# Another order of products in the feed-forward part of a two-layer transformer kernel, float32 on one core

## The chip, the cores and the metric

The kernel runs on one core of a Trainium2 chip. The core has a matrix engine (TensorE; PE in the profile, with its weight loads as PEld), two engines that work on rows of 128 partitions (VectorE, called DVE, and ScalarE, called ACT), a general one (GpSimd, called POOL), and SyncE (SP), which here only asks for transfers. Each engine takes its instructions strictly in order; they wait for each other by semaphores. Transfers (DMA) are asked for on a queue of SP or of POOL and carried out by 16 DMA engines that all queues share.

The metric is the device time of one execution in microseconds, the median of the runs.

## The reference, cut to what matters

All arrays are float32. There are two layers (DEPTH = 2); the sequence is S = 512 rows, the width D = 1024, the hidden width FFN = 2816. The change touches only the second half of each layer, the feed-forward network (FFN):

```python
for l in range(DEPTH):
    ...                                  # token mixer: three branches, gates, w_out
    x = layer_norm(ALPHA * x + mix, ln1_g[l], ln1_b[l])

    u = einsum('bsd,df->bsf', x, w_ffn_in[l])          # 512 x 1024 by 1024 x 5632
    u_gate, u_up = split(u, 2, axis=-1)
    ffn = einsum('bsf,fd->bsd', silu(u_gate) * u_up, w_ffn_out[l])   # 512 x 2816 by 2816 x 1024
    x = layer_norm(ALPHA * x + ffn, ln2_g[l], ln2_b[l])
```

## The kernel before, in words

**Numbers as pairs.** A float32 operand is carried as a pair of rounded float32r tiles, hi and lo. hi is a cast on ACT (L106 or L108 for activations, L154 or L259 for weights), lo = x − hi is a subtraction on DVE (L112 or L114, L155 or L260). A product of two pairs takes three matmuls (`mm3`, L121 to L124): hi·hi, hi·lo, lo·hi.

**Weights.** A weight block of 128 x 2048 floats (1 MB) is loaded into one of four staging buffers `st` (NSTAGE = 4), then cast and subtracted into one of three pairs `wh`, `wl` (AHEAD = 3). `run_items` fetches the weights of later items while fewer than three pairs are ready or in use. A staging buffer comes free when the subtraction has read it (and, where it keeps a running sum, after its last use); a pair when the last matmul of its product is done.

**Seven products.** Most of the FFN is done in blocks by a Strassen-Winograd scheme with seven products instead of eight: m1, y, x, m2, v, g, h (`u_two`, from L728). Each is 24 matmuls (two column halves j, four contraction tiles, three matmuls). x, g and h add onto the PSUM banks in which m1 was made, one after the other, v onto those of y. What a bank holds after g is read on DVE (`gg`, L760: `c = c22 - bank`), and only then may h write the same bank. The weights are sums of quarters of a weight matrix. `Chain` makes them one after the other in one staging buffer: SP loads (L174), and POOL adds the next quarter with an accumulating DMA (L178) as soon as the last sum has been split. `Close` keeps two or three quarters loaded (a, d, e) and adds on DVE (L233, L239). `ahead_a` and `ahead_c` ask for a weight early; they are called from the groups of an item (below).

**Stages.** The hidden columns are 22 tiles of 128. Sixteen come from four first-stage problems p, q, r, u (`u_fin`; Chain, Close, Chain, Close) of 512 gate and 512 up columns each. `gate_half` (L1200: tanh on ACT L1202, then DVE L1203) and `gated` (DVE L1211) make silu(gate)·up. `s_turn` (L1214) turns the result by eight PE transposes into two banks (L1223) and copies them on ACT (L1225). `s_ready`, `s_differ`, `s_sums`, `s_rest` (class `Twins`, L292 to L332) form the sums that the second stage takes as its other operand, a pair for each product, by casts and DVE operations (L322, L324 among them). The second stage has two output groups o and w (`fout_items`, both Chain) over four pairs of tiles each; their banks are added to the residual z by `plus` (L1295 the first time, L1297 later). The z tiles are loaded again from memory in o's m1 (`load_res`, eight loads of 256 KB).

The other six tiles (16 to 21) are plain: `u_ffn_first` (16, 17) and `u_ffn` (18 to 21), 48 matmuls each, and `ffn_done` (L1190) does tanh, gate and the split into a pair `hid[i]` at once. `fout_rest(0)` and `fout_rest(1)` multiply them by the last rows of w_ffn_out into the left and right 512 output columns. `fout_rest(0)` is two items, one for each weight block, with four banks open over both; `fout_rest(1)` (`chase`) takes both blocks, row tile by row tile, and each row tile's normalisation follows it.

**Order.** The order of products is a list written by hand (L1363 to L1379) of pairs (weights, function) with groups of further work. `run_items` (L550) issues an item's matmuls and, through `between`, one group after each of its halves. So the list sets the order of issue; a scheduler then fixes a static order on each engine, and that order is what runs.

Of the kernel before, what the change touches and what calls it, by code (L numbers as in the profile page):

```python
# [15 lines left out]
ALU = mybir.AluOpType  # L16
# [40 lines left out]
def trunk(ctx, tc, x_in, xT_in, w_in, ret_norm_g, da_norm_g, lq1, lk1, lq2, lk2, w_a, w_b, w_c, b_merge, w_out,  # L57
# [25 lines left out]
    def bank(name="ps"):  # L83
        return psp.tile([P, 512], F32, tag="ps", name=name)
# [276 lines left out]
    def proj_N(act, wts, t, ps, k0=0, start=True, stop=True):  # L361

        sl = slice(P * t, P * t + P)
        rows = [(wt, k) for wt in wts for k in range(wt.nk)]
        for i, (wt, k) in enumerate(rows):
            a = act[k0 + i]
            mm3(ps, a.hi[:, sl], a.lo[:, sl], wt.hi[:, k], wt.lo[:, k], start and i == 0, stop and i == len(rows) - 1)
# [84 lines left out]
    def bcast_rows(src):  # L452

        r = [g(name="bc") for _ in range(2)]
        for hf in range(2):
            nc.sync.dma_start(r[hf], src[:, 512 * hf:512 * hf + 512].to_broadcast([P, 512]))
        return r
# [145 lines left out]
    def layer(l):  # L603
# [586 lines left out]
        def ffn_done(i, pg, pu):  # L1190
            t = g(name="fth")
            nc.scalar.activation(t, pg, AF.Tanh, scale=0.5)
            nc.vector.scalar_tensor_tensor(t, t, 1.0, pg, op0=ALU.add, op1=ALU.mult)
            nc.vector.tensor_mul(t, t, pu)
            hid[i] = Pair("hid")
            split(hid[i], t, scale=0.5)

        nat, half = {}, {}

# [14 lines left out]
        def s_turn(pb, hf):  # L1214

            def fn():
                rows = [nat.pop((pb, 2 * hf + j)) for j in range(2)]
                for fp in range(2):
                    ps = bank("ph")
                    for i in range(2):  # L1220
                        for j in range(2):
                            o, c = 256 * i + P * j, P * (2 * fp + i)
                            nc.tensor.transpose(ps[:, o:o + P], rows[j][:, c:c + P], ident)  # L1223
                    t = half[pb, hf, fp] = g(name="hf")
                    nc.scalar.activation(t, ps, AF.Copy, scale=0.5)  # L1225
            return fn
# [3 lines left out]
        def s_ready(gi, fp):  # L1230
            def fn():
                pa, pc, k = 2 * gi, 2 * gi + 1, 8 * gi + 2 * fp
                tw = twins[gi, fp] = Twins(half.pop((pa, 0, fp)), half.pop((pa, 1, fp)))
                tw.ready(half.pop((pc, 0, fp)))
                hid[k], hid[k + 1] = tw.each
            return fn

        def s_differ(gi, fp):
            def fn():
                twins[gi, fp].difference(half.pop((2 * gi + 1, 1, fp)))  # L1240
            return fn

        def s_sums(gi, fp):
            def fn():
                twins[gi, fp].sums()
            return fn

        def s_rest(gi, fp):
            def fn():
                twins.pop((gi, fp)).rest()  # L1250
            return fn

        def s_x1(k):
# [29 lines left out]
        def u_ffn(i):  # L1283
            def fn(wt):
                pg = proj_T(x1T, wt, 0)
                pu = proj_T(x1T, wt, P)
                ffn_done(i, pg, pu)
            return [ffn_spec(i)], fn

        def plus(t, hf, ps, op, final=False):  # L1290

            z = x1["z"][t][hf]
            if (t, hf) in x2["fresh"]:
                x2["fresh"].remove((t, hf))
                nc.vector.scalar_tensor_tensor(z, z, ALPHA, ps, op0=ALU.mult, op1=op)  # L1295
            else:
                nc.vector.tensor_tensor(z, z, ps, op=op)  # L1297
            if final:
                x2["n"].stats(t, hf)

        def fout_items(gi):

            r0, kh = GROUPS[gi]
            hv = Chain(w_ffn_out[l], r0, kh)
            w = {}

            def it(name, *adds):
                def fn(wt):
                    if name == "m1" and gi == 0:
                        load_res(saved[2 * l])  # L1310
                        x2["fresh"] = {(t, hf) for t in range(NT) for hf in range(2)}
                    on = {"x": "m1", "g": "m1", "h": "m1", "v": "y"}.get(name, name)
                    for j in range(2):
                        w[on, j] = product([hid[r0 + k] for k in range(kh)], name, j, wt, w.pop((on, j), None))
                        for i, hf, op in adds:
                            plus(2 * i + j, hf, w[on, j], op)
                        if name in ("m2", "v", "h"):
                            w.pop((on, j))
                return [getattr(hv, name)], fn

            add, sub = ALU.add, ALU.subtract
            return {"c": hv.ahead_c, "m1": it("m1", (0, 0, add)), "y": it("y", (1, 1, add)), "x": it("x", (0, 1, sub)),
                    "m2": it("m2", (0, 0, add)), "v": it("v", (0, 1, add)), "g": it("g", (1, 1, sub)), "h": it("h", (1, 0, add))}

        def fout_rest(hf):


            banks = {}
            specs = rows_of(w_ffn_out[l], 512 * hf, REST, FT - REST)

            def block(kb):
                def fn(wt):
                    if kb == 0:
                        x2["n"] = Norm(x1["z"], v["g2"], v["b2"], bcast_rows(ln2_g[l:l + 1]),
                                       bcast_rows(ln2_b[l:l + 1]), xTs[l + 1], out if last else saved[2 * l + 1], xfs[l + 1])
                        banks[0] = [bank("pf") for _ in range(NT)]
                    end = kb == len(specs) - 1
                    for t in range(NT):
                        proj_N(hid, [wt], t, banks[0][t], REST + 4 * kb, kb == 0, end)
                        if end:  # L1340
                            plus(t, 0, banks[0][t], ALU.add, True)
                return fn

            def chase(*wts):
                n = x2["n"]
                for t in range(NT):
                    ps = bank("pf")
                    proj_N(hid, wts, t, ps, REST)
                    if t in (1, 2) and not last:
                        n.transposes(t - 1)  # L1350
                    plus(t, 1, ps, ALU.add, True)
                    if last:
                        n.finish(t)
                    else:
                        n.normalise(t)
                        if t == 2:
                            n.to_T(0)

            return [([sp], block(kb)) for kb, sp in enumerate(specs)] if hf == 0 else [(specs, chase)]

        p, q, r, u = u_fin(0, Chain), u_fin(1, Close), u_fin(2, Chain), u_fin(3, Close)
        o, w = fout_items(0), fout_items(1)
        for (specs, fn), *groups in [  # L1363
            (u_ffn_first([16, 17]), [s_natural(0)], [s_x1(0)]), (p["m1"], [s_x1(1)], [s_x1(2)]),
            (u_ffn(18), [s_x1(3), s_natural(1)], [p["c"]]), (p["m2"], [s_natural(2)], [s_natural(3)]), (p["y"],),
            (p["v"], [q["a"]]), (u_ffn(19),), (p["x"],), (q["m1"],), (p["g"], [s_turn(0, 0)]), (p["h"],),
            (q["y"], [q["c"]]), (q["v"], [s_turn(0, 1)]), (q["m2"],), (q["x"],), (r["m1"],), (q["g"], [s_turn(1, 0)]), (q["h"],),
            (r["y"],), (r["m2"], [s_turn(1, 1)], [r["c"]]), (r["v"], [u["a"]]), (r["x"],), (u["m1"],), (r["g"], [s_turn(2, 0)]),
            (r["h"], [s_ready(0, 0)], [s_ready(0, 1)]),
            (u["y"], [u["c"]]), (u["v"], [s_turn(2, 1)]), (u["m2"],), (u["x"],),  # L1370
            (o["m1"], [s_differ(0, 0)], [s_differ(0, 1)]), (u["g"], [s_turn(3, 0)]), (u["h"], [s_sums(0, 0)], [s_sums(0, 1)]),
            (o["m2"],), (o["y"], [s_turn(3, 1)], [o["c"]]), (u_ffn(20), [s_rest(0, 0)], [s_rest(0, 1)]), (o["v"], [s_ready(1, 0)], [s_ready(1, 1)]),
            (o["x"],), (w["m1"], [s_differ(1, 0)], [s_differ(1, 1)]), (o["g"],), (o["h"], [s_sums(1, 0)], [s_sums(1, 1)]),
            (w["m2"], [s_rest(1, 0)], [s_rest(1, 1)]), (w["y"], [w["c"]]), (u_ffn(21),), (w["v"],), (w["x"],),
            (w["g"],), (w["h"],),
        ]:
            item(specs, fn, *groups)
        for it in fout_rest(0) + fout_rest(1):
            item(*it)  # L1379

        def hook(b):
            x2["n"].transposes_of(1, b)
# [56 lines left out]
```

## Time and profile before

| | us |
|---|---|
| median of 3 runs | 1890.52 (1889.6 to 1891.29) |
| profiled execution, its own time | 1891.41 |
| its span | 1889.6 |
| window 602 to 940 (FFN of layer 0): PE busy | 333.69 of 338.00 |
| window 1542 to 1882 (FFN of layer 1): PE busy | 334.96 of 340.00 |
| window 1882 to 1889.6 (behind the last matmul): PE busy | 0.00 of 7.60 |

The profile is of one execution. Busy time of an engine is the time in which it executes; a wait is put down to the instruction whose semaphore came last. In the rows, `out<-in` gives tiles by the program's names, L is a line of the kernel, and `[2.43 <-DVE tc L760]` behind an instruction says that its engine had been idle for 2.43 us and that L760 on DVE ended the wait. The row of an item in the list of waits reads: who waited, for whom, us in total, how many times, the longest. The granted clock (PEclk) is a share of full speed. Matmuls overlap in the pipeline: one lasts 0.39 us, and the next starts 0.23 us after it.

### The profile page before, as it was taken

The numbers are of one execution on the slowest core, as the hardware profiler recorded it, in microseconds if no ns is written. First come the engines' busy times: TensorE is split into PE (matmuls) and PEld (weight loads), VectorE is DVE, ScalarE is ACT, GpSimd is POOL, SyncE is SP. The second block draws the span as 40 slices with busy tenths as digits, with TensorE's granted clock in tenths as the row PEclk, the third lists the DMA queues.
The fourth block names the chain that finished last, engine by engine and source line by source line (L and its number), as shares of the span: only waits on it lengthen the run. The fifth ranks groups of instructions, "written<-read, shape, count | busy, mean of one in ns | idle before, by whom it ended". The sixth has DMA issues, their size and how long they took to land. (4 is left out here: it accounts for less than half of the span.)

```text
span 1889.6 us, 24024 instructions
## 1 busy us (share of the span) xinstructions
PE 1869.7 (99%) x9138; PEld 1573.4 (83%) x9138; DVE 1344.3 (71%) x2055; ACT 973.5 (52%) x1579; POOL 124.4 (7%) x149
## 2 busy tenths in 40 slices
PE   9999999999999999999999999999999999999998
PEld 7888888888888888778898888888888888887786
DVE  6767756577766876688687778566776668757886
ACT  5545545566634454554255546455766345445540
POOL 2000000000001001010010000000000010010100
PEclk9999999999999999999999999999999999999999
DMA  9585443432155668698366944533322646686971
GB/s 287 164 280 144 122 162 107 123 122 69 57 183 142 152 192 201 170 231 205 129 194 171 285 112 135 167 114 99 123 68 82 194 115 174 174 212 189 220 191 45
DMA packets 220851, 297.69 MB, mean 158 GB/s; under 512 B 8516, under 2 KB 115104, under 8 KB 220736
## 3 DMA queue, kind: packets, MB, share of 16 engines
q1 hardware_dynamic: 192512, 241.20, 38.4%
q0 software_dynamic: 28224, 54.95, 17.1%
q8 instruction: 72, 1.18, 0.3%
q14 instruction: 43, 0.35, 0.1%
HBM read 273.00 MB, written 23.12 MB: 157 GB/s over the span
## 5 line engine op out<-in xcount | busy, mean ns | idle before, releaser
L122 PE MATMUL pt<-xTh,wh 128*128 128x512 f32 (+1 forms) x1072 | 397.2, 372 | 0.4 <-ACT wh L154 0.4
L123 PE MATMUL pt<-xTl,wh 128*128 128x512 f32 (+1 forms) x1072 | 393.5, 367 | 1.9 <-DVE xTl L112 1.9
L124 PE MATMUL pt<-xTh,wl 128*128 128x512 f32 (+1 forms) x1072 | 393.6, 368 | 0.0
L260 DVE TENSOR_TENSOR wl<-st,wh 128x2048 fp32r<-128x2048 f32 x126 | 288.3, 2289 | 143.5 <-ACT wh L259 143.3
L259 ACT CAST wh<-st 128x2048 fp32r<-128x2048 f32 x126 | 241.1, 1913 | 181.5 <-PE pf L124 91.1
L155 DVE TENSOR_TENSOR wl<-st,wh 128x1024 fp32r<-128x1024 f32 (+1 forms) x204 | 219.1, 1094 | 82.5 <-ACT wh L154 76.3
L154 ACT CAST wh<-st 128x1024 fp32r<-128x1024 f32 (+1 forms) x204 | 188.3, 949 | 161.4 <-PE pf L124 58.9
L123 PEld LDWEIGHTS pt<-xTl,wh 128*128 128x128 f32 x1072 | 202.3, 189 | 34.1 <-DVE xTl L112 2.3
L124 PEld LDWEIGHTS pt<-xTh,wl 128*128 128x128 f32 x1072 | 202.0, 188 | 33.7
L122 PEld LDWEIGHTS pt<-xTh,wh 128*128 128x128 f32 x1072 | 202.0, 189 | 33.0 <-ACT wh L154 1.0
L122 PE MATMUL pf<-wh,xTh 128*128 128x512 f32 x336 | 132.4, 394 | 6.1 <-DVE tc L760 4.9
L123 PE MATMUL pf<-wl,xTh 128*128 128x512 f32 x336 | 131.6, 392 | 0.0
L124 PE MATMUL pf<-wh,xTl 128*128 128x512 f32 x336 | 131.6, 392 | 0.0
L122 PE MATMUL pf<-wh,s43h 128*128 128x512 f32 x224 | 88.5, 395 | 0.0
L122 PE MATMUL pf<-wh,s12h 128*128 128x512 f32 x224 | 87.5, 391 | 0.0
L123 PE MATMUL pf<-wl,s43h 128*128 128x512 f32 x224 | 87.3, 390 | 0.0
L124 PE MATMUL pf<-wh,s43l 128*128 128x512 f32 x224 | 87.3, 390 | 0.0
L123 PE MATMUL pf<-wl,s12h 128*128 128x512 f32 x224 | 87.3, 390 | 0.0
L124 PE MATMUL pf<-wh,s12l 128*128 128x512 f32 x224 | 87.1, 390 | 0.0
L122 PEld LDWEIGHTS pf<-wh,xTh 128*128 128x128 f32 x336 | 63.5, 189 | 21.6 <-ACT wh L259 5.7
L745 ACT COPY tc<-pf 128x512 f32<-128x512 f32 x84 | 47.6, 588 | 60.5 <-PE pf L124 53.8
L124 PEld LDWEIGHTS pf<-wh,xTl 128*128 128x128 f32 x336 | 63.5, 189 | 13.3
(317 smaller groups left out, 3704.8 us busy)
## 6 DMA issues: line engine op xcount, KB each, us to landing
st<-in_w_in SPq DMA_DIRECT2D x60, 1024.0 KB, 5.2
st<-in_w_ffn_in SPq DMA_DIRECT2D x36, 1024.0 KB, 6.4
st<-in_w_ffn_in POOLq DMA_DIRECT2D x24, 1024.0 KB, 9.0
st<-in_w_ffn_out SPq DMA_DIRECT2D x20, 1024.0 KB, 6.5
st<-in_w_in SPq DMA_DIRECT2D x32, 512.0 KB, 5.2
st<-in_w_ffn_out POOLq DMA_DIRECT2D x16, 1024.0 KB, 9.0
st<-in_w_in POOLq DMA_DIRECT2D x12, 1024.0 KB, 10.9
th<-th SPq DMA_DIRECT2D x48, 256.0 KB, 5.0
```

The source lines that it names most:

```text
L122: nc.tensor.matmul(ps, lh, rh, start=start, stop=False, skip_group_check=onto)
L123: nc.tensor.matmul(ps, lh, rl, start=False, stop=False, skip_group_check=onto)
L124: nc.tensor.matmul(ps, ll, rh, start=False, stop=stop, skip_group_check=onto)
L154: return [nc.scalar.copy(self.hi[:, a:b], self.st[:, a:b]), nc.vector.tensor_sub(self.lo[:, a:b], self.st[:, a:b], f(self.hi[:, a:b]))]
L155: nc.vector.tensor_sub(self.lo[:, a:b], self.st[:, a:b], f(self.hi[:, a:b]))]
L259: nc.scalar.copy(self.hi, st)
L260: nc.vector.tensor_sub(self.lo, st, f(self.hi))
L745: nc.scalar.copy(t[to, j], ps)
```

## The change

1. **Order of products.** In p, q, r, u and o a product of the next problem (or, for o, of w) is put between g and h: p.g, q.y, p.h; q.g, r.m2, q.h; r.g, u.v, r.h; u.g, o.y, u.h; o.g, w.m2, o.h. w.g and w.h remain neighbours. The items around them and the groups of turns, twin sums and early loads move to other places in the list.
2. **Plain tiles stay unsplit.** `ffn_done` keeps the product itself, `hid[i] = t`. A new step `s_hid` makes the pairs: tiles 16, 17, 18 in the item of tile 21, and 19, 20, 21 in w.v.
3. **Plain rows, first half.** `fout_rest(0)` becomes one item `plain` with both weight blocks: for each of the four row tiles one bank, 18 matmuls, `plus`, `between`. It stands between w.x and w.g; `fout_rest(1)` stays last. Since w.h now comes after it, `plus` takes the statistics of z's left half after `plain` for row tiles 0 and 1 and after w.h for row tiles 2 and 3.

The kinds and numbers of instructions stay the same. From L1196 on, line numbers of the changed kernel are one lower up to its `s_rest` (L1223 becomes L1222, L1211 becomes L1210).

```diff
@@ ffn_done
-            hid[i] = Pair("hid")
-            split(hid[i], t, scale=0.5)
+            hid[i] = t
@@ behind s_rest
+        def s_hid(*ids):
+            def fn():
+                for i in ids:
+                    t, hid[i] = hid[i], Pair("hid")
+                    split(hid[i], t, scale=0.5)
+            return fn
@@ fout_items
-                            plus(2 * i + j, hf, w[on, j], op)
+                            plus(2 * i + j, hf, w[on, j], op, gi == 1 and name == "h")
@@ fout_rest
-            banks = {}
             specs = rows_of(w_ffn_out[l], 512 * hf, REST, FT - REST)
-            def block(kb):
-                def fn(wt):
-                    if kb == 0:
-                        x2["n"] = Norm(...)
-                        banks[0] = [bank("pf") for _ in range(NT)]
-                    end = kb == len(specs) - 1
-                    for t in range(NT):
-                        proj_N(hid, [wt], t, banks[0][t], REST + 4 * kb, kb == 0, end)
-                        if end:
-                            plus(t, 0, banks[0][t], ALU.add, True)
-                return fn
+            def plain(*wts):
+                x2["n"] = Norm(...)
+                for t in range(NT):
+                    ps = bank("pf")
+                    proj_N(hid, wts, t, ps, REST)
+                    plus(t, 0, ps, ALU.add, t < NT // 2)
+                    between()
...
-            return [([sp], block(kb)) for kb, sp in enumerate(specs)] if hf == 0 else [(specs, chase)]
+            return specs, (plain, chase)[hf]
@@ the list
-            (p["v"], [q["a"]]), (u_ffn(19),), (p["x"],), (q["m1"],), (p["g"], [s_turn(0, 0)]), (p["h"],),
-            (q["y"], [q["c"]]), (q["v"], [s_turn(0, 1)]), (q["m2"],), (q["x"],), (r["m1"],), (q["g"], [s_turn(1, 0)]), (q["h"],),
-            (r["y"],), (r["m2"], [s_turn(1, 1)], [r["c"]]), (r["v"], [u["a"]]), (r["x"],), (u["m1"],), (r["g"], [s_turn(2, 0)]),
-            (r["h"], [s_ready(0, 0)], [s_ready(0, 1)]),
-            (u["y"], [u["c"]]), (u["v"], [s_turn(2, 1)]), (u["m2"],), (u["x"],),
-            (o["m1"], [s_differ(0, 0)], [s_differ(0, 1)]), (u["g"], [s_turn(3, 0)]), (u["h"], [s_sums(0, 0)], [s_sums(0, 1)]),
-            (o["m2"],), (o["y"], [s_turn(3, 1)], [o["c"]]), (u_ffn(20), [s_rest(0, 0)], [s_rest(0, 1)]), (o["v"], [s_ready(1, 0)], [s_ready(1, 1)]),
-            (o["x"],), (w["m1"], [s_differ(1, 0)], [s_differ(1, 1)]), (o["g"],), (o["h"], [s_sums(1, 0)], [s_sums(1, 1)]),
-            (w["m2"], [s_rest(1, 0)], [s_rest(1, 1)]), (w["y"], [w["c"]]), (u_ffn(21),), (w["v"],), (w["x"],),
-            (w["g"],), (w["h"],),
+            (p["v"], [q["a"]]), (u_ffn(19),), (p["x"],), (q["m1"],), (p["g"], [s_turn(0, 0)]), (q["y"],), (p["h"],),
+            (q["v"], [q["c"]]), (q["m2"], [s_turn(0, 1)]), (q["x"],), (r["m1"],), (q["g"], [s_turn(1, 0)]), (r["m2"], [r["c"]]), (q["h"],),
+            (r["y"], [u["a"]]), (r["v"], [s_turn(1, 1)]), (u["m1"],), (r["x"],), (u["y"], [s_ready(0, 0)]), (r["g"], [s_turn(2, 0)]),
+            (u["v"], [s_ready(0, 1), u["c"]]), (r["h"],),
+            (u["m2"],), (o["m1"], [s_turn(2, 1)]), (u["x"], [s_differ(0, 0)], [s_differ(0, 1)]), (o["m2"],),
+            (u["g"], [s_turn(3, 0)], [o["c"]]), (o["y"],), (u["h"], [s_sums(0, 0)], [s_sums(0, 1)]),
+            (o["v"], [s_rest(0, 0)], [s_rest(0, 1)]), (u_ffn(20), [s_turn(3, 1)]), (o["x"], [s_ready(1, 0)], [s_ready(1, 1)]),
+            (w["m1"], [s_differ(1, 0)]), (o["g"], [s_differ(1, 1)], [w["c"]]), (w["m2"], [s_sums(1, 0)]), (o["h"], [s_sums(1, 1)]),
+            (w["y"], [s_rest(1, 0)]), (u_ffn(21), [s_rest(1, 1)], [s_hid(16, 17, 18)]), (w["v"], [s_hid(19, 20, 21)]), (w["x"],),
+            (fout_rest(0),), (w["g"],), (w["h"],), (fout_rest(1),),
-        for it in fout_rest(0) + fout_rest(1):
-            item(*it)
```

More of the change, by code (lines that the diff above doesn't have):

```diff
@@ L1325, in fout_rest @@
         def fout_rest(hf):
-            banks = {}
             specs = rows_of(w_ffn_out[l], 512 * hf, REST, FT - REST)
-            def block(kb):
-                def fn(wt):
-                    if kb == 0:
-                        x2["n"] = Norm(x1["z"], v["g2"], v["b2"], bcast_rows(ln2_g[l:l + 1]),
-                                       bcast_rows(ln2_b[l:l + 1]), xTs[l + 1], out if last else saved[2 * l + 1], xfs[l + 1])
-                        banks[0] = [bank("pf") for _ in range(NT)]
-                    end = kb == len(specs) - 1
-                    for t in range(NT):
-                        proj_N(hid, [wt], t, banks[0][t], REST + 4 * kb, kb == 0, end)
-                        if end:
-                            plus(t, 0, banks[0][t], ALU.add, True)
-                return fn
+            def plain(*wts):
+                x2["n"] = Norm(x1["z"], v["g2"], v["b2"], bcast_rows(ln2_g[l:l + 1]),
+                               bcast_rows(ln2_b[l:l + 1]), xTs[l + 1], out if last else saved[2 * l + 1], xfs[l + 1])
+                for t in range(NT):
[3 more added lines that the diff above has]
+                    between()
             def chase(*wts):
```

## The prediction, made before the changed kernel ran

> **What bounds the kernel now.** I read the page first: the shares of the engines, the slices, the chain that ended last.
>
> ```profile
> span 1889.6 us, 24024 instructions
> PE 1869.7 (99%) x9138; PEld 1573.4 (83%) x9138; DVE 1344.3 (71%) x2055; ACT 973.5 (52%) x1579; POOL 124.4 (7%) x149
> PEclk9999999999999999999999999999999999999999
> ```
>
> TensorE is busy 99% of the span at full clock, and the change keeps all 9138 matmuls. So only two things can move the time: gaps in PE's stream, and the clock behind a gap. The profiled execution took 1891.4 us, 1.8 more than its span and 0.9 more than the median of the runs shown (1890.52). I sum on 1891.4 and take the 0.9 off at the end. About 0.2%, 3.8 us, is what a measurement can tell from no change.
>
> Next the list of PE's waits: who was waited for, us in total, how often, the longest.
>
> ```profile
> PE pf L122 <- DVE tc L760: 4.9, 2, 2.5
> ...
> PE pf L123 <- DVE wl L260: 1.2, 2, 0.7
> ...
> PE pf L122 <- DVE z L1297: 0.5, 2, 0.2
> ```
>
> These three, once per layer each, are the waits inside the FFN's products and output groups: 4.9 + 1.2 + 0.5 = 6.6 us. The first is the one that the change aims at. Product h writes onto the bank of g, and L760 (tc = c22 − g) must have read it. There are six g,h pairs per layer (p, q, r, u, o, w), and only one of them waits. The timeline shows which, r's; a bracket is idle time and its releaser:
>
> ```profile
> 759.18 1.91 ACT L259 CAST wh<-st 128x2048 fp32r<-128x2048 f32 x1 [8.43 <-DMA st<-in_w_ffn_in]
> ...
> 761.13 2.29 DVE L260 TENSOR_TENSOR wl<-st,wh 128x2048 fp32r<-128x2048 f32 x1 [5.40 <-ACT wh L259]
> 763.91 2.29 DVE L260 TENSOR_TENSOR wl<-st,wh 128x2048 fp32r<-128x2048 f32 x1 [0.49 <-ACT wh L259]
> 766.12 1.28 DVE L760 TENSOR_TENSOR tc<-tc,pf 128x512 f32<-128x512 f32 x2
> ...
> 760.75 1.03 PE L1223 MATMUL ph<-ident,tc 128*128 128x128 f32 x8
> 761.54 0.48 PE L122 MATMUL pf<-wh,s43h 128*128 128x512 f32 x1
> ...
> 766.95 0.47 PE L122 MATMUL pf<-wh,xTh 128*128 128x512 f32 x1 [2.43 <-DVE tc L760]
> ...
> 1707.70 0.47 PE L122 MATMUL pf<-wh,xTh 128*128 128x512 f32 x1 [2.52 <-DVE tc L760]
> ...
> 763.45 0.37 SPq L174 DMA_DIRECT2D st<-in_w_ffn_in  x1
> ```
>
> L760 is short. It is late because DVE serves in order and two weight subtractions L260 stand before it, and those are late because ACT's cast idled 8.43 us for a load. The root is a late load; g,h adjacency is only where it hurts. Two more things are read here: SP issues the next load 763.45 − 759.18 = 4.27 us after a cast begins (cast, subtract, buffer free), and two L760 end within 1.28, so short DVE operations follow each other at 0.60. Eight transposes occupy PE 761.54 − 760.75 = 0.79.
>
> What a stall costs beyond itself stands in the busy time by windows (length, then PE, PEld, DVE, ACT, POOL busy, granted clock, DMA share, GB/s):
>
> ```profile
> 767.00:771.00 4.00, 4.00 (x11) 3.17 (x12) 2.60 (x2) 0.00 (x0) 1.28 (x1) 0.57 0.23 87
> 1708.00:1712.00 4.00, 4.00 (x19) 3.29 (x18) 2.98 (x4) 1.11 (x2) 1.28 (x1) 1.00 0.20 77
> 900.00:920.00 20.00, 20.00 (x90) 16.57 (x89) 8.26 (x10) 3.68 (x5) 0.00 (x0) 1.00 0.52 167
> ```
>
> After layer 0's stall the clock was 0.57 for 4 us, (1 − 0.57) × 4.0 = 1.7 us lost; after the equally long one in layer 1 it stayed at 1.00. The Trainium skill, page "TensorE: Matmul & The Clock Gate", section "HAM oscillation — how this bites in real kernels", gives as its abstract rule that PE should have no idle gap above about 3.4 us; by it a 2.43 us gap would cost no clock, and the sum below would lose its 1.7 and end at about 1895.4. The first of these windows differs from that, so the measurement decides, and I count one such drop among long stalls of this kind.
>
> **What the change removes.** A product of 24 matmuls comes between g and h in p, q, r, u and o. Its length, from eight steps of 0.2275:
>
> ```profile
> 1702.98 0.39 PE L122 MATMUL pf<-wh,s43h 128*128 128x512 f32 x1
> ...
> 1704.80 0.39 PE L124 MATMUL pf<-wh,s43l 128*128 128x512 f32 x1
> ```
>
> 24 × 0.2275 = 5.46 us, more than the 2.52 missing, so r's wait goes; that L760 would be later still by more than 2.9 us has nothing for it. u and o.m2's neighbourhood is reordered too, so I also give away the other two waits. Gain: 6.6 + 1.7 = 8.3 us at most, over both layers. The other four pairs had no wait to remove.
>
> **What it adds: stall A.** The late load is not removed, and products pulled forward bring their weights forward while only four staging buffers exist. In the new order of the instructions, when r.h ends (call it T0) all four are held: three by u's sums (d, e, c), one by o's running sum. So o.m2's load goes out only when u.x's weights have been split, and that cast waits for the weight buffer that r.h releases. SP's issue: T0 + 0.2 + 4.27 = T0 + 4.5. Its landing:
>
> ```profile
> 707.05 1.28 POOL L178 DMA_DIRECT2D st<-in_w_ffn_in  x1 [22.67 <-DVE wl L260]
> ...
> 712.18 0.37 SPq L174 DMA_DIRECT2D st<-in_w_ffn_in  x1
> ...
> st<-in_w_ffn_in SPq DMA_DIRECT2D x1, 1024.0 KB, 7.4
> ...
> st<-in_w_ffn_out SPq DMA_DIRECT2D x20, 1024.0 KB, 6.5
> ```
>
> The first two issues are 5 us apart, as a POOL accumulation and o.m2's load will be, and that load (the third line, DMA issues in the window 712 to 713) took 7.4; the median of its kind is 6.5. Behind it queue, in order, on ACT the cast and on DVE the subtraction (4.24 from cast begin to subtract end, as above: 761.13 + 2.29 − 759.18), and then the last gate operations of problem r:
>
> ```profile
> L155 DVE TENSOR_TENSOR wl<-st,wh 128x1024 fp32r<-128x1024 f32 x14 | 16.9, 1220 | 1.3 <-ACT wh L154 1.1
> L1211 DVE TENSOR_TENSOR fth<-tc,fth 128x512 f32<-128x512 f32 x8 | 5.5, 686 | 0.1
> L1203 DVE SCALAR_TENSOR_TENSOR fth<-fth,pf 128x512 f32<-128x512 f32 x8 | 5.5, 683 | 3.2 <-ACT fth L1202 3.1
> L1295 DVE SCALAR_TENSOR_TENSOR z<-z,pf 128x512 f32<-128x512 f32 x8 | 5.3, 681 | 0.8 <-DMA z<-saved 0.8
> L322 DVE TENSOR_TENSOR ta<-ta,hf 128x512 f32<-128x512 f32 x4 | 2.7, 686 | 0.0
> L324 DVE TENSOR_TENSOR hf<-hf,ta 128x512 f32<-128x512 f32 x4 | 2.7, 684 | 0.0
> ```
>
> Two L1203 and one L1211 at 0.60, with 0.1 for handing on, are 1.9. For a landing time L, problem r's second turn can transpose at T0 + 4.5 + L + 4.24 + 1.9 = T0 + 10.6 + L: 17.1 to 18.0. These transposes now stand inside u.x, behind 68 matmuls counted from r.h's end (u.m2 24, o.m1 24, 20 of u.x), so PE is there at 68 × 0.2275 = T0 + 15.5. Stall 1.6 to 2.5; alone on the queues L would be 5.2 and the stall 0.3. I take 2.2 per layer, nearer the 7.4 row because its neighbour is the same. In before, the same transposes stood after u.v, where nothing waited.
>
> **Stall B, at plain tile 20.** Let T1 be the end of o.m2's subtraction; A's transposes are released at T1 + 1.9. In the new order PE meets tile 20's first low-half matmul 102 matmuls and two sets of transposes later: T1 + 1.9 + 102 × 0.2275 + 2 × 0.79 = T1 + 26.7. Its weights' subtraction on DVE stands behind that of o.v's weights, and those are the last of what SP asks for after T1: o.c 1 MB, eight z tiles of 256 KB, o.v 1 MB, together 4.2 MB, while POOL moves two accumulations of 1 MB (o.c at about T1 + 5, o.y's at about T1 + 12). The transfer view for three windows, POOL alone (747 to 753), both (754.5 to 757), SP alone (758.5 to 761), and the eight z issues of before:
>
> ```profile
> DMA packets 621, 1.24 MB, mean 207 GB/s; under 512 B 16, under 2 KB 16, under 8 KB 621
> ...
> DMA packets 320, 0.66 MB, mean 262 GB/s; under 512 B 0, under 2 KB 0, under 8 KB 320
> ...
> q0 software_dynamic: 160, 0.33, 70.4%
> q1 hardware_dynamic: 160, 0.33, 39.2%
> ...
> DMA packets 515, 1.02 MB, mean 408 GB/s; under 512 B 17, under 2 KB 17, under 8 KB 515
> ...
> 800.55 3.30 SPq L450 DMA_DIRECT2D z<-saved  x7
> ...
> st<-in_w_ffn_in SPq DMA_DIRECT2D x1, 1024.0 KB, 5.2
> ```
>
> The last line is a load alone (763 to 764): 5.2, of which 2.6 is moving 1.05 MB at 400, so some 2.1 to 2.6 is latency. Alone SP would land all at T1 + 2.1 + 10.5 = T1 + 12.6. When both move they share 262 evenly; each POOL megabyte then takes 8 us, in which SP moves 1.05 MB instead of 3.2, a loss of 5.4. One accumulation inside: T1 + 18.0; both: T1 + 23.4. The second is asked for before 18.0, so nearly all of it lies inside: I take T1 + 22. Cast and subtraction, T1 + 26.2; then two L1295, two L322, one L324 at 0.60, 29.3 with hand-over; then tile 20's first half subtraction 1.22 (L155): T1 + 30.5. Stall 30.5 − 26.7 = 3.8 per layer; 0 with one accumulation inside, 5.2 with both wholly.
>
> **C.** o.v's own operands (the split of Twins' v) are behind these on ACT and DVE: 0 to two operations of 0.6; I take 0.6.
>
> **Costed at nothing.** Splits of hid 16 to 21 moved to two places in the second group: six casts and six subtractions that fall where the window 900 to 920 shows DVE busy 8.3 and ACT 3.7 of 20 us; if that cover were gone, six subtractions of 0.68, 4.1 us. The plain rows as one item of four times 18 matmuls before w.g, with its two weight blocks and the four broadcast loads of the norm moved past w.g and w.h on SP: PE has the same work, the last item stays last and its row loop keeps its order, so the tail behind the last matmul is the same. w.g and w.h stay adjacent, and waited for nothing in before. Natural rows and Quarters sums are not moved.
>
> **Sum.** 1891.4 − 8.3 + 2 × (2.2 + 3.8 + 0.6) + 1.7 for one clock drop among the new long stalls = 1898.0; less 0.9, 1897.1: some 6.6 us slower.
>
> **Rivals.** *SP keeps its rate* (the other side): o.v's weights land with at most one accumulation inside, that is by T1 + 18.2, so B is 0 and C with it, and A is 1.6 with L = 6.5, no clock drop: 1891.4 − 8.3 + 3.2 − 0.9 = 1885.4. For it: the 6.5 median includes loads among POOL's. Against: both accumulations are issued before 18.0. *B short*: A in full, the landing near T1 + 19.5, B about 1.2, one drop: 1891.4 − 8.3 + 2 × 3.4 + 0.8 (half a drop's chance) − 0.9 = 1889.8, no measurable change. *Each long stall halves the clock*: four stalls, three drops more: 1897.1 + 5.1 = 1902.2. *h waits all the same*: then its 4.9 + 1.7 come back on top, 1904; only if DVE's queue before L760 grows by a product's length, for which no row speaks.
>
> **Chances.** Forecast 0.60, its own range 1893 to 1901; SP keeps its rate 0.17; B short 0.17; clock or h worse 0.06. Leaving out the fastest case's 0.17 and a little above gives 1888 to 1902.5. Faster 0.17, same 0.17, slower 0.66.
>
> **What would show it.** In the waits of the changed kernel: the row for DVE tc L760 gone; a new PE ph wait of about 2 us, twice, for DVE's L1210 (the shifted L1211); a wait of about 4, twice, of tile 20's matmuls for the L154 cast or L155 subtraction; SP's load for o.m2 4.5 us after r.h ends; about 262 GB/s shared by two queues for 14 us or more before tile 20. I am wrong if the landing of o.v's weights comes before T1 + 18.2, or if o.m2's load goes out before u.x's split.

## The result, and the profile after

| | us |
|---|---|
| changed kernel, median of 5 runs | 1898.77 (1897.71 to 1899.02) |
| kernel before, median of 5 runs beside it | 1891.29 (1889.6 to 1894.22) |
| ratio, 95% interval | 1.0038 [1.0023, 1.0052] |
| span of the profiled execution, before / after | 1889.6 / 1896.8 |

The change made the kernel about 7 us slower. The page of the changed kernel and its list of PE's waits, the lines that answer to those of before:

```profile
span 1896.8 us, 23994 instructions
PE 1870.7 (99%) x9138; PEld 1574.8 (83%) x9138; DVE 1344.4 (71%) x2055; ACT 973.2 (51%) x1579; POOL 124.5 (7%) x149
...
PE pt L122 <- ACT wh L154: 6.7, 3, 3.5
PE ph L1222 <- DVE fth L1210: 4.5, 2, 2.4
...
PE pt L124 <- DVE wl L155: 1.1, 2, 0.5
...
PE pf L122 <- ACT qvh L106: 0.5, 1, 0.5
...
PE pf L124 <- DVE qvl L112: 0.2, 1, 0.2
```

The rows for tc L760, for wl L260 and for z are gone. In their place stand the turn (4.5 us) and tile 20 (3.5 and 2.2 us for its cast, 1.1 for its subtraction; the third time in the L154 row, 1.0 us, lies at the kernel's start), with 0.7 for o.v's operands behind it.

The turn, layer 0, in the timeline (start, length, engine, line; in brackets the idle time and its releaser):

```profile
785.72 0.37 SPq L174 DMA_DIRECT2D st<-in_w_ffn_out  x1
...
792.84 1.91 ACT L259 CAST wh<-st 128x2048 fp32r<-128x2048 f32 x1 [9.47 <-DMA st<-in_w_ffn_out]
...
794.78 2.29 DVE L260 TENSOR_TENSOR wl<-st,wh 128x2048 fp32r<-128x2048 f32 x1 [7.20 <-ACT wh L259]
796.99 1.28 DVE L1202 SCALAR_TENSOR_TENSOR fth<-fth,pf 128x512 f32<-128x512 f32 x2
798.19 1.29 DVE L1210 TENSOR_TENSOR fth<-tc,fth 128x512 f32<-128x512 f32 x2
...
798.93 0.44 PE L1222 MATMUL ph<-ident,fth 128*128 128x128 f32 x2 [2.10 <-DVE fth L1210]
```

r.h ends at 781.3. SP asks for o.m2's weights 4.4 us later, they land 7.0 us after that, ACT casts, DVE subtracts, and only then come the gate operations for which the transposes wait. This is the predicted chain, link by link.

Tile 20, layer 0:

```profile
803.08 0.38 SPq L174 DMA_DIRECT2D st<-in_w_ffn_out  x1
814.84 1.13 SPq L150 DMA_DIRECT2D st<-in_w_ffn_in  x2
...
809.87 1.28 POOL L178 DMA_DIRECT2D st<-in_w_ffn_out  x1 [5.76 <-DVE wl L260]
...
812.49 2.29 DVE L260 TENSOR_TENSOR wl<-st,wh 128x2048 fp32r<-128x2048 f32 x1
...
818.28 2.29 DVE L260 TENSOR_TENSOR wl<-st,wh 128x2048 fp32r<-128x2048 f32 x1 [2.31 <-ACT wh L259]
...
822.89 0.69 DVE L324 TENSOR_TENSOR hf<-hf,ta 128x512 f32<-128x512 f32 x1
...
826.02 2.00 ACT L154 CAST wh<-st 128x1024 fp32r<-128x1024 f32 x2 [7.77 <-DMA st<-in_w_ffn_in]
...
827.10 2.36 DVE L155 TENSOR_TENSOR wl<-st,wh 128x1024 fp32r<-128x1024 f32 x2 [3.52 <-ACT wh L154]
...
827.12 0.50 PE L122 MATMUL pt<-xTh,wh 128*128 128x512 f32 x1 [3.51 <-ACT wh L154]
...
828.38 0.80 PE L124 MATMUL pt<-xTh,wl 128*128 128x512 f32 x1 [0.53 <-DVE wl L155]
```

This is not the predicted chain. o.v's subtraction (818.28) is done at 820.6; DVE does five short operations more, the last of them L324, and then stands idle from 823.6 for 3.52 us before L155. PE reaches tile 20 at the same 823.6 (827.12 less 3.51), so the queue behind o.v is not what PE waits for. ACT's bracket names the wait: tile 20's own weights. SP asked for them (L150) at 814.84, at once when u.h's subtraction (812.49 + 2.29) had given a staging buffer back, and they landed 11 us later, while POOL's accumulations moved.

The clock, in the windows behind these stalls:

```profile
828.00:832.00 4.00, 3.62 (x9) 2.94 (x10) 4.00 (x7) 4.00 (x7) 0.00 (x0) 0.57 0.21 66
...
1740.00:1744.00 4.00, 1.60 (x8) 1.44 (x9) 4.00 (x7) 2.53 (x3) 0.00 (x0) 0.89 0.50 158
1744.00:1748.00 4.00, 4.00 (x16) 3.27 (x15) 3.60 (x5) 2.42 (x3) 1.30 (x1) 0.68 1.03 387
```

One drop in each layer: 0.43 x 4 = 1.7 us, and (0.11 + 0.32) x 4 = 1.7 us. The balance of the two profiled executions: 6.6 of old waits and 1.7 of clock gone, 4.5 + 6.7 + 0.7 = 11.9 of new waits and 3.4 of clock come, together +7.0; the spans differ by 7.2.

### The profile page after: what moved, and what is told of

Same layout as the page of the kernel before. It is cut to its first block, busy times and chain, and to the rows that moved or that the text cites. A ratio compares the mean times of both kernels' runs of the same rounds, so it can differ in the third digit from the quotient of the medians.

```text
span 1896.8 us, 23994 instructions
## 1 busy us (share of the span) xinstructions
PE 1870.7 (99%) x9138; PEld 1574.8 (83%) x9138; DVE 1344.4 (71%) x2055; ACT 973.2 (51%) x1579; POOL 124.5 (7%) x149
## 5 line engine op out<-in xcount | busy, mean ns | idle before, releaser
L260 DVE TENSOR_TENSOR wl<-st,wh 128x2048 fp32r<-128x2048 f32 x126 | 288.5, 2290 | 157.5 <-ACT wh L259 149.7
L155 DVE TENSOR_TENSOR wl<-st,wh 128x1024 fp32r<-128x1024 f32 (+1 forms) x204 | 218.6, 1095 | 72.7 <-ACT wh L154 66.7
L154 ACT CAST wh<-st 128x1024 fp32r<-128x1024 f32 (+1 forms) x204 | 188.0, 948 | 151.5 <-issue 46.9
```

The source lines that it names most:

```text
L154: return [nc.scalar.copy(self.hi[:, a:b], self.st[:, a:b]), nc.vector.tensor_sub(self.lo[:, a:b], self.st[:, a:b], f(self.hi[:, a:b]))]
L155: nc.vector.tensor_sub(self.lo[:, a:b], self.st[:, a:b], f(self.hi[:, a:b]))]
L260: nc.vector.tensor_sub(self.lo, st, f(self.hi))
```

## The experiments

Every ratio is to the kernel before in runs on the same chip; that kernel's median lay between 1891.3 and 1893.1 us in these comparisons.

### Which product helps, and why

**One exchange alone.** In the kernel before, u.y is put between r.g and r.h:

```diff
-            (r["h"], [s_ready(0, 0)], [s_ready(0, 1)]),
-            (u["y"], [u["c"]]), (u["v"], [s_turn(2, 1)]), (u["m2"],), (u["x"],),
+            (u["y"], [u["c"]]), (r["h"], [s_ready(0, 0)], [s_ready(0, 1)]),
+            (u["v"], [s_turn(2, 1)]), (u["m2"],), (u["x"],),
```

> The kernel before, with one pair of neighbours exchanged: u.y comes between r.g and r.h; nothing else of the change. Theory (the wait on L760 came from two late weight subtractions ahead of it on DVE, and one product of 5.46 us covers it): both L760 waits (4.9 us) go and the clock drop behind one of them (1.7) with them; u.y's weights are there in time, as r.h's landed at 759.1 and the product starts at 764.4. 1891.3 - 4.9 - 1.7 = 1884.7. Rival (the late load takes its toll in any order: u.y waits for its weights in place of h): a new wait of 2 us or more per layer before u.y and 1889 or more.

Measured: 1883.60 us, 0.9952 [0.994, 0.9965]. No wait on L760 is left, and only 0.4 us of waits inside the products and output groups of both layers. So the gain at which the change aims exists, 9.1 us where 8.3 were predicted, and one exchange of neighbours has all of it. Its DVE rows show more than cover:

```profile
755.77 2.28 DVE L260 TENSOR_TENSOR wl<-st,wh 128x2048 fp32r<-128x2048 f32 x1
761.17 2.29 DVE L260 TENSOR_TENSOR wl<-st,wh 128x2048 fp32r<-128x2048 f32 x1 [3.12 <-ACT wh L259]
763.38 0.68 DVE L760 TENSOR_TENSOR tc<-tc,pf 128x512 f32<-128x512 f32 x1
764.63 0.69 DVE L760 TENSOR_TENSOR tc<-tc,pf 128x512 f32<-128x512 f32 x1 [0.57 <-PE pf L124]
```

u.y's subtraction now stands first and is over at 758; only r.h's, whose load is late, is left before L760. In the kernel before r.h's came first, and u.y's, stood behind it, although its weights were long there: in this run its cast began at 752.90 and had waited for PE to free a weight pair, not for a load. L760 now ends at 764.1 and 765.3, and r.g itself ends at about 764.4.

**The two splits alone.** So a further run exchanged nothing but these two splits: products keep the order r.g, r.h, u.y, and the weights of u.y are fetched before those of r.h. Apart from the fetch loop, which takes item k + 1 before item k where k is r.h, the kernel is the one before; on ACT and DVE the only change of order is that of these two casts and two subtractions in each layer. Of its edit, the lines that exchange the two (cut):

```diff
+        turn = list(range(len(items)))
+        for k in swap:
+            turn[k], turn[k + 1] = turn[k + 1], turn[k]
```

> The kernel before with its order of products kept (r.g, r.h, u.y); only the two weight splits of r.h and u.y change places on ACT and DVE. Theory (the wait on L760 comes from u.y's subtraction, held back behind r.h's, whose load is late; the product put between g and h helps by the changed order of the two splits, not by its length): u.y's split is done by 758, r.h's subtraction ends at 763.4 as before, the first L760 at 764.1, while r.g ends at 764.4, the second at about 765.3; waits on L760 0.3 us or less, no clock drop, 0.9952 to 0.997 of the kernel before. Rival (it is the 5.46 us of cover that counts): an L760 wait of 2 us or more per layer stays, 1.000.

Measured: 1885.62 us, 0.9964 [0.995, 0.9978]; no wait on L760 (here L763):

```profile
757.06 2.28 DVE L260 TENSOR_TENSOR wl<-st,wh 128x2048 fp32r<-128x2048 f32 x1
761.57 2.30 DVE L260 TENSOR_TENSOR wl<-st,wh 128x2048 fp32r<-128x2048 f32 x1 [2.22 <-ACT wh L259]
763.77 0.68 DVE L763 TENSOR_TENSOR tc<-tc,pf 128x512 f32<-128x512 f32 x1
```

This settles r's pair: with g and h still neighbours the wait is gone. No distance between them is needed; an early weight was held up behind a late one in two in-order queues. Whether distance without the exchange would have done as well for this pair, no run shows (for u's pair, in the section on the plain tiles, it does).

**The other pairs.** In the kernel before, h of p, q, u and o changes places with the item behind it (p.g, q.y, p.h; q.g, r.y, q.h; u.g, o.m2, u.h; o.g, w.m2, o.h); the groups keep their order; r.g and r.h stay neighbours.

> The kernel before with a product between g and h for p, q, u and o, made by exchanging h with the item behind it; r.g and r.h stay neighbours. Theory (only r's pair had a wait to remove): no gain; the L760 waits of 2.4 to 2.5 us stay, the time within 2 us of the kernel before, or slower where an exchange brings weights forward. Rival (each pair apart is worth something, a hidden wait of 0.2 us and more): 2 us or more faster.

Measured: 1897.89 us, 1.0024 [1.0014, 1.0035]. No gain, as the theory has it, but the L760 waits of r did not stay at 2.4 to 2.5: they grew to 4.1 and 6.6. In layer 0 ACT's cast of r.h's weights now idles 11.13 us for its load, in place of 8.43: the exchanges made the late load later.

```profile
PE pf L122 <- DVE tc L760: 10.6, 2, 6.6
```

**r.g and r.h neighbours again, in the changed kernel.**

```diff
-            (u["v"], [s_ready(0, 1), u["c"]]), (r["h"],),
+            (r["h"],), (u["v"], [s_ready(0, 1), u["c"]]),
```

> The changed kernel, with r.h put back directly behind r.g, so u.v stands behind both. Theory (in the changed order the two subtractions ahead of r's L760 are no longer late, L760 follows r.g by 0.3 us, so the product between g and h covers nothing here): no wait on L760 above 0.7 us per layer, the waits at the turn and at tile 20 stay: 1898.8 within 1.5. Rival (it is the product between g and h that removed the wait): 2.4 us per layer back and a clock drop of 1.7 with one of them: 1903.6 to 1905.3.

Measured: 1909.52 us, 1.0090 [1.0076, 1.0104]. On the disputed point the theory holds: no wait on L760, so in the changed order too the product between r.g and r.h covers nothing. The time is another matter, slower than either theory said. The turn's wait is gone, and one of 10.7 to 10.8 us has come in each layer:

```profile
815.11 1.92 ACT L259 CAST wh<-st 128x2048 fp32r<-128x2048 f32 x1 [1.93 <-DMA st<-in_w_ffn_out]
830.61 1.99 ACT L154 CAST wh<-st 128x1024 fp32r<-128x1024 f32 x2 [13.58 <-DMA st<-in_w_ffn_in]
...
833.50 0.62 ACT L106 CAST qvh<-hf 128x512 fp32r<-128x512 f32 x1
...
834.18 0.80 PE L122 MATMUL pf<-wh,qvh 128*128 128x512 f32 x1 [10.74 <-ACT qvh L106]
```

o.v waits for its small cast qvh, and that stands on ACT behind the cast of tile 20's weights, for which ACT stood still for 13.58 us. It is the same late load, asked for at 815.6 here. It landed 15 us later, in place of 11, just behind two accumulations that POOL issued at 813, and it has more queued behind it.

### The wait at the turn

**The turn one product later.**

```diff
-            (u["m2"],), (o["m1"], [s_turn(2, 1)]), (u["x"], [s_differ(0, 0)], [s_differ(0, 1)]), (o["m2"],),
+            (u["m2"],), (o["m1"],), (u["x"], [s_differ(0, 0)], [s_differ(0, 1)]), (o["m2"], [s_turn(2, 1)]),
```

> The changed kernel, with the second turn of problem r moved by one product, from o.m1 to o.m2. Theory (the wait of 2.1 and 2.4 us at that turn is made by its place: its gate operations stand on DVE behind o.m2's late subtraction, and PE gets there 2 us early): the wait goes, with the clock drop that followed it in layer 1: 1898.8 - 4.5 - 1.7 = 1892.6; tile 20, reached 2 us sooner, may take up to half of it back: up to 1896. Rival (the wait belongs to o.m2's weights and only changes its name): a wait of 2 us per layer before o.m2's first matmuls and 1898 or more.

Measured: 1898.96 us, 1.0038 [1.0026, 1.0051], the time of the changed kernel. The theory fails. The rival is right in the time and in that the wait only changes its name; the place it named, before o.m2's first matmuls, was wrong. Layer 0's waits, with tile 20's in the first row:

```profile
PE pt L122 <- ACT wh L154: 3.4, 1, 3.4
PE ph L1222 <- DVE z L1303: 1.5, 1, 1.5
PE pf L122 <- ACT wh L259: 1.2, 1, 1.2
```

The 2.1 us at the turn have become 1.2 + 1.5 us at u.g and at the next turn. What is late is o.m2's load and the weights behind it on ACT and DVE; the turn was only the first to meet it.

**The load asked for earlier.** Two early loads are asked for later, so that they hold no staging buffer when o.m2's load is due: o.c as in the run on tile 20 below, and u.c in o.m1's group.

```diff
-            (u["v"], [s_ready(0, 1), u["c"]]), (r["h"],),
-            (u["m2"],), (o["m1"], [s_turn(2, 1)]), (u["x"], [s_differ(0, 0)], [s_differ(0, 1)]), (o["m2"],),
+            (u["v"], [s_ready(0, 1)]), (r["h"],),
+            (u["m2"],), (o["m1"], [s_turn(2, 1), u["c"]]), (u["x"], [s_differ(0, 0)], [s_differ(0, 1)]), (o["m2"],),
```

> The changed kernel with the early load of o.g's weights in o.v's group (as the run that took tile 20's wait away) and, in addition, the early load of u.g's weights asked for in o.m1's group, behind o.m2's load. Theory (o.m2's load goes out only at 785.7 because u.c holds the fourth staging buffer; the wait at r's second turn is this load's): o.m2's load goes out at about 770, 15 us sooner, and the wait of 2.3 to 2.6 us at the turn goes; u.g's weights, now asked for at about 786, land with their accumulation at 802 to 807 and are split by 806 to 811, while PE wants them at about 804: a new wait of 2 to 7 us before u.g, so against 0.998 of the kernel before without this edit between 0.997 and 1.003. Rival (the wait at the turn is made by gate operations on DVE and by the turn's place, whenever o.m2's load lands): the 2.3 to 2.6 us stay.

Measured: 1899.55 us, 1.0036 [1.0024, 1.0048]. In layer 0:

```profile
769.30 0.37 SPq L174 DMA_DIRECT2D st<-in_w_ffn_out  x1
...
785.29 0.37 SPq L174 DMA_DIRECT2D st<-in_w_ffn_in  x1
...
805.53 0.49 PE L122 MATMUL pf<-wh,s43h 128*128 128x512 f32 x1 [1.69 <-ACT wh L259]
...
807.85 0.79 PE L123 MATMUL pf<-wl,s43h 128*128 128x512 f32 x1 [1.83 <-DVE wl L260]
```

o.m2's load goes out at 769.3 in place of 785.7, and the turn waits for nothing; u.c goes out at 785.3, and u.g waits 3.5 us (5.0 in layer 1). The mechanism is as stated, four buffers for five blocks. The time is 0.0006 above the bracket, with 3.1 us more waits before o.v.

### The wait at tile 20

```diff
-            (u["g"], [s_turn(3, 0)], [o["c"]]), (o["y"],), (u["h"], [s_sums(0, 0)], [s_sums(0, 1)]),
-            (o["v"], [s_rest(0, 0)], [s_rest(0, 1)]), (u_ffn(20), [s_turn(3, 1)]), (o["x"], [s_ready(1, 0)], [s_ready(1, 1)]),
+            (u["g"], [s_turn(3, 0)]), (o["y"],), (u["h"], [s_sums(0, 0)], [s_sums(0, 1)]),
+            (o["v"], [s_rest(0, 0)], [s_rest(0, 1), o["c"]]), (u_ffn(20), [s_turn(3, 1)]), (o["x"], [s_ready(1, 0)], [s_ready(1, 1)]),
```

> The changed kernel, with the early load of o.g's weights (o.c: 1 MB by SP and an accumulation of 1 MB by POOL) asked for in o.v's group in place of u.g's. Theory (tile 20's weights are asked for only at 814.8, when u.h's staging buffer comes free, because o.c holds the fourth one; they land 11 us later, with POOL's accumulations on the same DMA engines): tile 20's load is asked for 8 us or more earlier, its waits (4.0 and 2.7 us, with 0.6 behind them) go, and the clock drop of layer 0 that followed: 1898.8 - 7.3 - 1.7 = 1889.8; the wait at the turn stays at 2.1 to 2.4. Rival 1 (the prediction's own step: tile 20's subtraction stands on DVE behind that of o.v's weights, which the z tiles hold up): tile 20's wait stays at 3 to 4 us, 1897 or more. Rival 2 (o.g's weights are then late instead): a new wait before o.g, 1894 to 1900.

Measured: 1888.86 us, 0.9980 [0.9971, 0.9989]. Tile 20's load goes out 10.5 us earlier, all its waits are gone and none has come before o.g; the turn keeps its own.

```profile
PE ph L1222 <- DVE fth L1210: 5.0, 2, 2.6
...
804.38 1.02 SPq L150 DMA_DIRECT2D st<-in_w_ffn_in  x2
```

From 1.0038 to 0.9980 is 0.0058, 11 us, by the place of one early load (9.2 us between the two profiled spans), and it makes the changed order faster than the kernel before. As a test of the prediction's own chain for stall B (rival 1) it is weaker than it looks: the edit also takes o.c's load and accumulation from ahead of o.v's weights, whose load goes out at 798.5 in place of 803.1, so by that chain too the wait would have gone (it expected none with one accumulation inside). What refutes the chain is the trace of the changed kernel, where DVE stood idle while PE waited for tile 20's weights. How much of tile 20's lateness was the buffer and how much the accumulations beside its load, the run does not separate.

### The plain tiles

Parts 2 and 3 of the change were costed at nothing. Five runs took them apart. One constant of the kernel is named in what follows: all working tiles of 128 x 512 share one pool of 61 slots (NSLOT), and a plain tile takes one slot unsplit and two as a pair.

**Both parts on the order of before.** The list of before with `s_hid` in the items of tile 21 and w.v, and `fout_rest(0)` as one item before w.g:

```diff
-            (w["m2"], [s_rest(1, 0)], [s_rest(1, 1)]), (w["y"], [w["c"]]), (u_ffn(21),), (w["v"],), (w["x"],),
-            (w["g"],), (w["h"],),
+            (w["m2"], [s_rest(1, 0)], [s_rest(1, 1)]), (w["y"], [w["c"]]), (u_ffn(21), [], [s_hid(16, 17, 18)]), (w["v"], [s_hid(19, 20, 21)]), (w["x"],),
+            (fout_rest(0),), (w["g"],), (w["h"],), (fout_rest(1),),
```

> The kernel before with the change's second and third part alone (plain tiles split late; first half of the plain rows as one item before w.g), its order of products otherwise kept. Theory (both parts lie beside other work, as the prediction costed them): no change against the kernel before within 2 us, both L760 waits of 2.4 to 2.5 us still there. Rival (the whole of the added time, or a part of it, is theirs): 3 us or more slower, with waits behind tile 21.

Measured: 1898.44 us, 1.0035 [1.0024, 1.0046]: not nothing. The new wait is not where the plain rows are, but some 90 us earlier, at the first matmul of u.h (layer 0):

```profile
805.08 0.69 DVE L1301 SCALAR_TENSOR_TENSOR z<-z,pf 128x512 f32<-128x512 f32 x1 [2.85 <-PE ph L1222]
805.69 0.69 DVE L317 TENSOR_TENSOR ta<-hf 128x512 f32<-128x512 f32 x1
...
809.70 0.68 DVE L760 TENSOR_TENSOR tc<-tc,pf 128x512 f32<-128x512 f32 x1
...
809.81 0.62 ACT L106 CAST qyh<-ta 128x512 fp32r<-128x512 f32 x1 [2.79 <-DVE ta L317]
...
810.52 0.77 PE L122 MATMUL pf<-wh,xTh 128*128 128x512 f32 x1 [2.64 <-ACT qyh L106]
```

The profile puts it down to ACT's cast qyh, which came last, but this matmul reads xTh and wh, not qyh. What it needs is the bank of u.g, which L760 must have read: L760 ends at 810.38 and the matmul starts 0.14 later, as r.h starts 0.15 after its L760 in the kernel before; in layer 1, and in both layers of the late-split run below, the distance is 0.15 too. So it is a wait of a second g,h pair, u's, and the expectations that place it before o.y, two products later, follow the profile's name for it. L760 is late because DVE stood 2.85 us at a z update. In the kernel before, the same pair has cover that the list does not show: the scheduler put the first half of o.m2 (12 matmuls) between u.g and u.h, and there is none of it here.

```profile
808.74 0.61 PE L122 MATMUL pf<-wh,qm2h 128*128 128x512 f32 x2
...
812.22 0.39 PE L122 MATMUL pf<-wh,xTh 128*128 128x512 f32 x1
```

**Each part alone on the order of before.** `late_split` has only the late split, `plain_item` only the plain rows as one item.

> The kernel before with the late split of the plain tiles alone. Theory (each plain tile that waits unsplit holds one slot of the 61 in place of two, so work of the first stage gets its tiles earlier and takes another static order on DVE, where a z update now stands ahead of the twin difference that o.y waits for): the wait of 2.6 to 2.7 us per layer for ACT's qyh, before o.y, is there as in the run with both parts, and the time is 1.0035 of the kernel before, within 2 us. Rival (the plain rows' place, with their weight blocks earlier on SP, makes it): no such wait, and the time of the kernel before within 2 us.

> The kernel before with the plain rows' first half alone as one item before w.g; plain tiles split at once. Theory (the part is beside other work): no wait for qyh, both L760 waits of 2.4 to 2.5 us, the time of the kernel before within 2 us. Rival: as above the other way round, 1.0035.

Measured: late split 1906.84 us, 1.0072 [1.0058, 1.0086]; plain item 1893.11 us, 1.0002 [0.9993, 1.0011]. The plain item is free, as costed; its L760 waits were 2.3 and 4.1 us, and half of o.m2 still stands between u.g and u.h. The late split brings the wait at u.h (the first row), but not the time that its theory named: without the plain item there is a second wait, before w.g (the second row).

```profile
PE pf L122 <- ACT qyh L106: 5.2, 2, 2.6
PE pf L122 <- DVE z L1303: 4.9, 2, 2.5
```

With the L760 waits, 5.3, these are 15.4 us of waits, 8.8 more than in the kernel before. The clock dropped behind five of them and in the kernel before behind one: four drops more, some 7 us. Together that is nearly all of the 17.0 us between the two profiled spans.

**Both parts with r apart.** The run at 0.9952 with both plain parts added.

> The kernel before with u.y between r.g and r.h (the run at 0.9952) and both plain parts added. Theory (the late split brings its own wait before o.y, whatever stands between r.g and r.h): 0.9952 of the kernel before plus 2.6 us for each layer, 0.998, with no wait on L760. Rival (that wait is tied to the L760 wait, as both are DVE's order): no wait for qyh and 0.995 again.

Measured: 1883.39 us, 0.9957 [0.9945, 0.997], no wait for qyh. The theory fails: the late split has no price of its own. u.h stands directly behind u.g here too, but DVE does not stop at the z updates, and L760 ends at 808.0, 0.15 before u.h starts at 808.17.

**Late split undone in the changed kernel.** `ffn_done` splits at once, without `s_hid`.

> The changed kernel with the plain tiles split at once again, as in the kernel before. Theory (the late split is not on the path): the time of the changed kernel, 1.0038 of the kernel before, within 1.5 us, with the waits of 2.1 to 2.4 us at r's second turn and 2.7 to 4 us at tile 20. Rival (the late split made them, by six casts and subtractions less or more on ACT and DVE near tile 20): those waits differ by 2 us or more.

Measured: 1904.63 us, 1.0061 [1.0049, 1.0073]; the theory fails here too.

```profile
PE ph L1223 <- DVE fth L1211: 6.7, 2, 3.9
PE pf L122 <- ACT qvh L106: 3.9, 2, 2.0
```

The turn's wait has grown from 4.5 to 6.7 us and that for o.v's operands from 0.7 to 4.2, but tile 20's has shrunk from 6.7 to 1.5: together 12.4 us of waits in place of 11.9. The added time is the clock. In layer 0 it was 0.64 in the window 828 to 832 and 0.51 in 832 to 836, where the changed kernel had 0.57 and 1.00; over both layers, the missing share times PE's busy time in windows of 2 us is some 9 us in place of 3, and the spans differ by 5.9.

So the late split costs 14 us on one order (6 beside the plain item), nothing on a second, and saves some 4 us on a third (1.0061 against 1.0038). The runs show that it changes the static order of the engines, as with u.h above. That it does so by the number of free slots among the 61 is argued, not shown: it also moves six casts and six subtractions.

## Why the prediction was right, and where not

| term, both layers | predicted | measured |
|---|---|---|
| old waits and their clock drop removed | -8.3 | -8.3 |
| A, the turn | 4.4 | 4.5 |
| B, tile 20 | 7.6 | 6.7 |
| C, o.v's operands | 1.2 | 0.7 |
| clock drops | 1.7 | 3.4 |

- **Bound and direction: right.** PE's gaps and its clock carried the whole difference.
- **Removal: right in size, wrong in its reason.** The prediction said that 5.46 us of cover takes the wait away. The run with two splits exchanged shows that r's pair needs no cover, and the run with r.g and r.h neighbours in the changed order has no such wait either. The prediction saw that "the root is a late load", but did not see that u.y's early weight stood behind r.h's late one in the same queue, which was the part to mend. That the other pairs "had no wait to remove" holds for the order that ran, but u's had none because the scheduler had put half of o.m2 between its g and h; the late split took that away, and a wait of 2.6 us came.
- **A: right in chain and price.** The load was asked for 4.4 us after r.h's end (4.5 predicted) and landed in 7.0 (6.5 to 7.4). That the turn's place makes it was a later idea of mine, and fell; that four staging buffers make it is shown by the earlier load.
- **B: price right by chance, chain wrong.** The failed step is "its weights' subtraction on DVE stands behind that of o.v's weights, and those are the last of what SP asks for". Tile 20's own load was asked for after them, when u.h's buffer came free, and PE waited for that load. The landing was wrong as well: o.v's weights came at about 816.3, T1 + 19.2 with T1 = 797.1, not T1 + 22, and the two queues moved data together for some 7 us (within the windows of 2 us from 806 to 816), not 14. The prices (3.8, and 4.0 in layer 0) agree by chance; layer 1 had 2.7. Neither of the two signs of being wrong came, since 19.2 lies behind 18.2, so they would not have caught it. I had applied the buffer count to o.m2's load and not to the load that comes next.
- **Costed at nothing:** right for the plain item; for the late split wrong as a rule, since its price depends on the order that it meets. In the whole change it happened to help, by some 4 us, and by way of the clock.
- **Clock and the miss:** one drop more than counted, 1.7 us, against 1.3 us less of waits. That is 0.4 of the 1.7 us between 1897.1 and 1898.77. The kernel before was itself 0.8 us slower beside the changed one (1891.29) than in the runs shown (1890.52); the rest, 0.5, is within the spread of the runs.
- **Rivals.** "SP keeps its rate" did not come. The landing of o.v's weights was nearly that of "B short" (T1 + 19.5), but its wait of 1.2 us was not, since tile 20 did not depend on that landing.

Best of all kernels run is the one before with u.y between r.g and r.h, 1883.60 us; with both plain parts added it is the same, 1883.39. No wait over 0.2 us is left in its products and output groups.

## What to carry to other kernels

When a cheap operation is late on an in-order engine, look at what stands ahead of it and ask which of those was ready early: exchanging two splits was worth 0.4%, the rebuilt order of which it was a part cost 0.4%. Count staging buffers for every load after the one that was checked: a load asked for ahead of its use holds a buffer, and here its price was a wait of 2 to 4 us at an item that had nothing to do with it. Where a scheduler fixes the order, the list of issue is not the order that runs: half a product stood between u.g and u.h that the list did not have, and an edit elsewhere removed it. Compare the order of each engine before and after an edit before costing it at nothing. And where the profile names an instruction that the waiting one does not read, look for the one that it does read and that ended at the same time.

## What was not expected of the hardware

Below a certain length, a gap did not tell whether the clock drops. Gaps of 2.43 us (before, layer 0), 3.51 (after, tile 20, layer 0) and 2.40 (after, the turn, layer 1) were followed by a loss of 1.7 us each; gaps of 2.52 (before, layer 1) and 2.10 (after, the turn, layer 0) by none. Over the FFN windows of all fourteen profiles, each of the twelve gaps of 2.78 us and more was followed by a drop, and those from 1.97 to 2.75 us went both ways. Nor is the loss always 1.7 us: behind the longest wait at the turn in the run that splits the plain tiles at once (3.94 us) the clock was 0.50 in the window 1748 to 1752 and still 0.73 in 1752 to 1756. The Trainium skill, page "TensorE: Matmul & The Clock Gate", section "Part 1: The HAM clock gate (the "warmup" mystery)", says that the activity window is free-running, so that the same kernel can fare differently by its phase; that agrees with such gaps going both ways, while the 3.4 us that it gives as the length of a gap with consequences lies above two of the first three gaps named here. No run here shows the window itself.
